# Moving the first output projection of each layer ahead of the attention of the following query tiles

## The chip, the cores and the metric

The kernel runs on one core of one Trainium2 chip. The metric is the device time of one execution in microseconds (us). The engines are called PE (matrix multiply; PEld is its weight load), DVE, ACT and POOL (elementwise work) and SP (the queue from which this kernel issues its data transfers). All inputs and the result lie in the device's main memory.

## The reference: what is computed

A two-layer transformer trunk over 1024 latent tokens and 256 context tokens, width 1024. Each layer has two halves.

First half: normalise (RMS) and modulate the tokens, project them (`w_in`), and compute three groups of mixers side by side. Group A is a gated mix within chunks of 128 positions. Group B is attention of 8 query heads in a window of 128 positions to each side, plus the context. Group C is differential attention: 4 heads, each with two softmax maps over all 1280 keys, whose difference weights the values. The three outputs are concatenated and go through one output projection (`w_out`), gated and added to the tokens:

```python
x = x + g1 * (jnp.concatenate([out_a, out_b, out_c], axis=-1) @ w_out[i])
x = x + g2 * conv_ffn(modulate(rms_norm(x, norm2_g[i]), sh2, sc2), w_up[i], conv_w[i], conv_b[i], w_down[i])
```

Second half: normalise again, then a gated MLP with 2816 inner channels and a convolution of width 3 along the tokens. Context tokens run through layer 0 in full, and in layer 1 only as keys and values.

## The kernel before, in words

**Tokens and groups.** A tile is 128 tokens: 0 to 7 are latent, 8 and 9 context. Attention works on pairs of tiles: (0,1), (2,3), (4,5), (6,7) and, in layer 0, (8,9). The output projection and the MLP work on three token groups per layer. In layer 0, `G0[0]` is tile 0 and the context (384 columns), `G0[1]` is tiles 1 to 3, `G0[2]` is tiles 4 to 7. In layer 1, `G1[0]` is tiles 0 and 1 (256 columns), `G1[1]` is tiles 2 to 4, `G1[2]` is tiles 5 to 7.

**Attention.** `attn_b(L, pair)` is group B for one pair of tiles: two units, one for each key head. `attn_c(L, hd, pairs)` is group C for one head and a list of pairs: one unit for each pair. It loads the head's keys and values once for the list (`Kc`, `Vc`). A unit of C runs, for each of its two tiles and two maps, three score matmuls into the accumulator tile `S` (L679), the running maximum on DVE (L483), the exponential on ACT (L682); then per tile the difference of the two maps on DVE (L689); then transposes into `T` (L714), copies to `PT` (L716) and the value matmuls into `O` (L705). The copy `on<-O` (L725) comes once per unit, so its count tells how many C units are done. For B, the transposes are L596, the value matmuls L606, and `ob<-O` (L619) comes once per unit. Each unit stores its result into the array `o_s` in main memory. There is one `O` tile, two `S` tiles and four tiles for exponentials.

**Output projection and norms.** `prep(L, G, ...)` takes one token group: it reads `o_s` back into `oT` in four parts (L786; the first part is group A, the next two are B, the last is C), loads `w_out` in eight slices of 128 output channels, runs 24 matmuls per slice (8 row blocks times 3 terms; L130, `z<-oT,wsp`), adds into `xg` (L807), and then normalises each 128 tokens: square on ACT (L200), sums on DVE (L203, L204), the power on POOL (L211), scaling on DVE (L217), modulation on ACT (L227), splitting into two parts (L228, L109). The MLP of that group can begin when all its norms are there.

**MLP.** `mlp(L, G, ...)` runs 22 steps f. Each loads two slices of `w_up`, runs `z<-h,wsp` matmuls, convolution and gate, and ends in `g<-t` (L864, once per step). The down projection (`z<-g,wsp`) of four finished steps is put between. All weights, of `w_out`, `w_up` and `w_down` alike, pass through the same three raw and three split buffers (`raw`, `wsp`), and projections and MLP share the same two accumulator tiles `z`.

**The order.** The program text is not the order on the engines. A scheduler that simulates the program picks, for each engine, the ready instruction that stands first in the text, and the resulting order on each engine is fixed. Text order is therefore a rank: what stands earlier wins when both are ready, and what stands later fills in. During the MLP of one group a hook at step f issues `prep` of the next group: `HK = (16, 13, 20, 12)`, so in layer 0 `prep(0, G0[1])` ranks in the middle of step 16 of the first MLP, and in layer 1 `prep(1, G1[1])` in the middle of step 20. Four steps ahead of that its `oT` loads are put into the text one by one.

Around the change, layer 0 has: the input projection with the attention of (8,9) and (0,1); then B and C of (2,3); `prep` of `G0[0]`; B and C of (4,5) and (6,7); the MLP of `G0[0]`. Layer 1 has: the input projection with the attention of (0,1); B and C of (2,3) and (4,5); `prep` of `G1[0]`; B and C of (6,7); the MLP of `G1[0]`.

Of the kernel before, what the change touches and what calls it, by code (L numbers as in the profile page):

```python
# [52 lines left out]
def trunk(ctx: ExitStack, tc: tile.TileContext, a: dict):  # L53
# [3 lines left out]
    def mkpool(name, bufs, side="left", space=None):  # L57
        kw = {"space": space} if space is not None else {}
        return tc.alloc_tile_pool(name=name, bufs=bufs, side=side, reuse_waits="tile", **kw)
# [51 lines left out]
    def wunit(src, nk, ncol, ws=ws, eng=dve):  # L111
        raw = wr.tile([P, nk, ncol], F32, tag="raw", name="raw")
        sp.dma_start(out=raw, in_=src.rearrange("(k p) c -> p k c", p=P))
        hl = ws.tile([P, 2, nk, ncol], F32R, tag="ws", name="wsp")
        act.activation(out=hl[:, 0], in_=raw, func=AF.Copy)  # L115
        if eng is pool and nk * ncol > 256:
            for k in range(nk):
                sub(eng, hl[:, 1, k], raw[:, k], hl[:, 0, k])
        else:
            sub(eng, hl[:, 1], raw, hl[:, 0])  # L120
        return hl

    def mm3(ps, w, h, nk, stat_w=True, first=True, last=True):

        for k in range(nk):
            for q, (i, j) in enumerate(TERMS):
                s = first and k == 0 and q == 0
                e = last and k == nk - 1 and q == 2
                if stat_w:
                    pe.matmul(ps, w(i, k), h(j, k), start=s, stop=e)  # L130
                else:
                    pe.matmul(ps, h(i, k), w(j, k), start=s, stop=e)  # L132
# [98 lines left out]
    def norm_tile(L, which, src, s, hi, lo, mkps, mkbig, f=None, ss=None, eng=pool, add='a'):  # L231
        norm_back(L, which, norm_front(src, mkps, mkbig, f, ss), s, hi, lo, eng, add)
# [536 lines left out]
    def attn_b(L, tiles, at, mkS, mkT, mkO):  # L769
        attend(units_b(L, tiles, at, mkS, mkT, mkO))  # L770

    def attn_c(L, hd, groups, at, mkS, mkT, mkO):
        attend(units_c(L, hd, groups, at, mkS, mkT, mkO))


    def prep_loads(L, G, p):

        wd = G["W"]
        xg = p.tile([P, KT, wd], F32, tag="xg", name="xg", bufs=1)
        oT = p.tile([P, 2, KT, wd], F32R, tag="h", name="oT", bufs=1)  # L780

        def load(k):
            for (xc, n, pieces) in G["op"]:
                for (tok, o, m, s) in pieces:
                    for h in range(2):
                        sp.dma_start(out=oT[:, h, k:k + 2, xc + o:xc + o + m].bitcast(F32),  # L786
                                     in_=o_s[L][h, k * P:k * P + 2 * P, tok:tok + m].rearrange("(c p) t -> p c t", p=P))

        return xg, oT, [lambda k=k: load(k) for k in range(0, KT, 2)]

    def prep(L, G, p, mp, pl=None, lo=dve):

        wd = G["W"]
        xg, oT, loads = pl or prep_loads(L, G, p)
        while loads:
            loads.pop(0)()
        if G["xh"]:
            dve.tensor_copy(xg[:, :, 0], xh)
        for (xc, n, pieces) in G["op"]:
            for ct in range(KT):  # L800
                w = wunit(a["w_out"][L][:, ct * P:ct * P + P], KT, P, eng=lo)
                ps = mkz()
                mm3(ps[:, :n], lambda j, k: w[:, j, k, :], lambda j, k: oT[:, j, k, xc:xc + n], KT)
                for (tok, o, m, s) in pieces:
                    xs = xg[:, ct, xc + o:xc + o + m]
                    sp.dma_start(out=xs, in_=x_s[:, ct, tok:tok + m])
                    dve.scalar_tensor_tensor(out=xs, in0=ps[:, o:o + m], scalar=mods[:, L, 16 + ct, s:s + 1], in1=xs,  # L807
                                             op0=ALU.mult, op1=ALU.add)
        hT = p.tile([P, 2, KT, wd], F32R, tag="h", name="h2", bufs=1)
        if G["xh"]:  # L810
            dve.tensor_copy(hT[:, :, :, 0:2], hal.bitcast(F32))
        big = lambda: mp.tile([P, KT, P], F32, name="nb", tag="nb", bufs=2)
        for i, (xc, hc, s) in enumerate(G["norm"]):
            norm_tile(L, 1, xg[:, :, xc:xc + P], s, hT[:, 0, :, hc:hc + P], hT[:, 1, :, hc:hc + P], mkU, big,
                      add=AN[L])

        def halo():
            if G["halo"] is not None:
                hc, xc = G["halo"]
                dve.tensor_copy(hal, hT[:, :, :, hc:hc + 2].bitcast(F32))  # L820
                dve.tensor_copy(xh, xg[:, :, xc])

        return xg, hT, halo
# [71 lines left out]
    def finish(L, G, xg, mp):  # L895
        if L < DEPTH - 1:
            for ct in range(KT):
                for (tok, xc, n) in G["out"]:
                    sp.dma_start(out=x_s[:, ct, tok:tok + n], in_=xg[:, ct, xc:xc + n])
            return  # L900
        for (tok, xc, n) in G["out"]:
            for o in range(0, n, P):
                m = min(P, n - o)
                ot = mp.tile([P, KT, P], F32, name="ot", tag="nb", bufs=2)
                for g in range(2):
                    px = mkT()
                    for k in range(4):
                        pe.transpose(px[:m, k * P:k * P + P], xg[:, 4 * g + k, xc + o:xc + o + m], ident)
                    if g:
                        dve.tensor_copy(ot[:m, 4:8], px[:m].rearrange("p (k t) -> p k t", k=4))  # L910
                    else:
                        act.activation(out=ot[:m, 0:4], in_=px[:m].rearrange("p (k t) -> p k t", k=4), func=AF.Copy)
                m16 = m - m % 16
                for r0, r1 in ((0, m16), (m16, m)):
                    if r1 > r0:
                        sp.dma_start(out=a["out"][0, tok + o + r0:tok + o + r1, :],
                                     in_=ot[r0:r1].rearrange("p k t -> p (k t)"))
# [15 lines left out]
    G1 = [dict(id="a", xh=False, W=256, op=[(0, 256, [(0, 0, 256, 0)])], norm=[(0, 0, 0), (128, 128, 0)],  # L933
               halo=(254, 255), segs=[(0, 256, [(0, 256, 0, 255, 0, 0)])], out=[(0, 0, 255)]),
          dict(id="b", xh=True, W=386, op=[(1, 384, [(256, 0, 384, 0)])], norm=nrm(3), halo=(384, 384),
               segs=[(0, 386, [(0, 386, 1, 385, 0, 0)])], out=[(255, 0, 384)]),
          dict(id="c", xh=True, W=386, op=[(1, 384, [(640, 0, 384, 0)])], norm=nrm(3), halo=None,
               segs=[(0, 386, [(0, 386, 1, 386, 0, 0)])], out=[(639, 0, 385)])]
# [13 lines left out]
    def mkz():  # L952
        zc[0] += 1
        if zc[1] and zc[0] % 2:
            return psS.tile([P, 512], F32, tag="S", name="zS")
        return psD.tile([P, 512], F32, tag="z", name="z")
# [103 lines left out]
    def attn(L, tiles):  # L1060
        for t in tiles:
            attn_b(L, t, at, mkS, mkT, mkO)
        for hd in range(4):
            attn_c(L, hd, tiles, at, mkS, mkT, mkO)
# [9 lines left out]
    M = mkpool("M0", 2, "right")  # L1074
    X2 = mkpool("X2", 1, "right")
    X1 = mkpool("X1", 1, "right")
    attn(0, [(2, 3)])
    x1 = prep(0, G0[0], X1, M)
    attn(0, [(4, 5), (6, 7)])

    def hook(f):
        ahead(0, G0[1], X2, f, HK[0], "x2")
# [2 lines left out]
    finish(0, G0[0], x1[0], M)  # L1085
    X1.release()
    at.release()
# [17 lines left out]
    M = mkpool("M1", 2, "left")  # L1105
# [52 lines left out]
    M = mkpool("M2", 2, "right")  # L1158
    X2 = mkpool("X5", 1, "right")
    X1 = mkpool("X4", 1, "right")  # L1160
    for t in A1[0]:
        attn_b(1, t, at, mkS, mkT, mkO)
    for hd in range(4):
        attn_c(1, hd, A1[0], at, mkS, mkT, mkO)
    x1 = prep(1, G1[0], X1, M)
    for t in A1[1]:
        attn_b(1, t, at, mkS, mkT, mkO)
    for hd in range(4):
# [6 lines left out]
    finish(1, G1[0], x1[0], M)  # L1175
    X1.release()
    at.release()
# [65 lines left out]
```

## Time and profile before

| | us |
|---|---|
| median of 3 runs | 3356.69 |
| lowest and highest | 3352.62, 3362.18 |
| the profiled execution | 3354.95 |
| its span, first to last instruction | 3353.1 |
| PE busy (94% of the span) | 3164.3 |
| DVE busy (70%) | 2342.6 |
| ACT busy (52%) | 1744.9 |
| POOL busy (26%) | 883.6 |

In the views, a group of instructions is written as line, engine, operation, tile written and tiles read. "x24" is a count. A window is a stretch of the span in us; for each engine it gives the busy time in it and the number of instructions. PEclk is the share of PE's full clock that was granted there. Matmuls overlap each other, so the busy time of PE counts a stretch once even where it is filled thinly.

### The profile page before, as it was taken

What the parts mean: (1) busy time and instruction counts of PE and PEld (TensorE: products, weight loads), DVE (VectorE), ACT (ScalarE), POOL (GpSimd) and SP (SyncE); (2) the same over time, 40 slices, a digit from 0 to 9 for tenths busy, and PEclk for the clock granted to TensorE, in tenths of its full rate; (3) what the DMA queues carried; (4) which work ended last, traced back from release to release, by engine and by line L of the source; (5) the groups of instructions that cost most, each with busy time, mean ns of one, the idle gap of its engine ahead of it and who ended that gap; (6) DMA issues with size and microseconds to landing.
All of it is one profiled execution on the core that took longest, in us unless ns stands there. A gap on an engine that the chain in (4) does not pass through costs nothing. (4 is left out here: it accounts for less than half of the span.)

```text
span 3353.1 us, 54588 instructions
## 1 busy us (share of the span) xinstructions
PE 3164.3 (94%) x19503; PEld 2753.6 (82%) x19503; DVE 2342.6 (70%) x5306; ACT 1744.9 (52%) x3059; POOL 883.6 (26%) x1170
## 2 busy tenths in 40 slices
PE   6999998999999899999999899999999989999999
PEld 3777556887888798989999777666887779999998
DVE  5776756756878785878677678647786685666666
ACT  3555546555555653646444345556665564454443
POOL 1545211222233550128001154222322323222000
PEclk8999999999999999999999899999999999999999
DMA  8655777344542853378243556445645446434433
GB/s 259 194 156 162 223 248 186 89 121 124 136 116 83 255 154 110 103 207 242 87 117 112 160 149 161 126 139 136 167 135 149 122 118 189 120 111 135 137 114 108
DMA packets 754127, 499.52 MB, mean 149 GB/s; under 512 B 81480, under 2 KB 697792, under 8 KB 753856
## 3 DMA queue, kind: packets, MB, share of 16 engines
q1 hardware_dynamic: 753856, 496.03, 51.7%
q8 instruction: 155, 2.54, 0.3%
q14 instruction: 116, 0.95, 0.1%
HBM read 432.48 MB, written 63.44 MB: 148 GB/s over the span
## 5 line engine op out<-in xcount | busy, mean ns | idle before, releaser
L130 PE MATMUL z<-h,wsp 128*128 128x386 f32 (+3 forms) x5280 | 871.7, 318 | 20.4 <-DVE t L854 10.2
L130 PEld LDWEIGHTS z<-h,wsp 128*128 128x128 f32 x5280 | 822.0, 190 | 36.4 <-issue 13.9
L115 ACT ACTIVATE wsp<-raw 128x1024 fp32r<-128x1024 f32 (+2 forms) x660 | 555.9, 845 | 442.1 <-PE z L130 179.0
L109 DVE TENSOR_TENSOR wsp<-raw,wsp 128x1024 fp32r<-128x1024 f32 (+2 forms) x516 | 565.9, 1099 | 121.3 <-ACT wsp L115 118.5
L130 PE MATMUL z<-g,wsp 128*128 128x386 f32 (+3 forms) x2640 | 463.5, 323 | 17.8 <-ACT wsp L115 5.7
L130 PEld LDWEIGHTS z<-g,wsp 128*128 128x128 f32 x2640 | 418.1, 192 | 35.8 <-issue 11.0
L132 PE MATMUL z<-wsp,h 128*128 128x512 f32 x1584 | 404.8, 402 | 13.0 <-ACT wsp L115 3.3
L109 POOL TENSOR_TENSOR wsp<-raw,wsp 128x128 fp32r<-128x128 f32 x528 | 253.9, 513 | 448.8 <-ACT wsp L115 397.2
L132 PEld LDWEIGHTS z<-wsp,h 128*128 128x128 f32 x1584 | 291.6, 191 | 79.9 <-ACT wsp L115 4.3
L130 PE MATMUL zS<-h,wsp 128*128 128x386 f32 (+1 forms) x2112 | 333.7, 313 | 8.1 <-DVE t L854 3.2
L130 PEld LDWEIGHTS zS<-h,wsp 128*128 128x128 f32 x2112 | 318.9, 190 | 10.9 <-ACT wsp L115 4.3
L847 ACT ACTIVATE t<-z,cw 128x386 f32<-128x386 f32 (+3 forms) x220 | 137.8, 627 | 209.8 <-PE z L130 208.6
L851 DVE SCALAR_TENSOR_TENSOR t<-z,cw,t 128x255 f32<-128x255 f32 (+3 forms) x264 | 132.5, 502 | 144.6 <-ACT t L847 144.2
L682 ACT ACTIVATE ec<-ec,nmc 128x1280 f32<-128x1280 f32 (+1 forms) x144 | 182.1, 1265 | 52.1 <-DVE ec L483 51.0
L170 POOL TENSOR_TENSOR mev<-mev,mtr 128x512 f32<-128x512 f32 x112 | 175.8, 1583 | 124.6 <-ACT mtr L169 121.7
L130 PE MATMUL z<-oT,wsp 128*128 128x384 f32 (+2 forms) x1056 | 200.0, 336 | 4.9 <-DMA oT<-o_s 3.4
L130 PE MATMUL zS<-g,wsp 128*128 128x386 f32 (+1 forms) x1056 | 184.4, 319 | 14.9 <-ACT wsp L115 4.3
L483 DVE TENSOR_SCALAR_CACHE_REDUCE ec<-S,nmc 128x512 f32<-128x512 f32 (+1 forms) x256 | 156.7, 612 | 56.0 <-PE S L679 52.7
L879 DVE SCALAR_TENSOR_TENSOR xg<-z,mods,xg 128x384 f32<-128x384 f32 (+5 forms) x288 | 140.4, 501 | 75.8 <-PE z L130 74.7
L130 PEld LDWEIGHTS z<-oT,wsp 128*128 128x128 f32 x1056 | 176.1, 188 | 15.1 <-issue 4.9
L370 POOL TENSOR_TENSOR rs<-ss,cst 128x8 f32<-128x8 f32 (+1 forms) x76 | 119.5, 1572 | 259.5 <-DVE ss L368 187.7
L579 POOL TENSOR_SCALAR dgb<-cst,ls 128x128 f32<-128x128 f32 x144 | 89.2, 632 | 372.7 <-PE T L616 182.3
(248 smaller groups left out, 4848.1 us busy)
## 6 DMA issues: line engine op xcount, KB each, us to landing
raw<-in_w_up_dram SPq DMA_DIRECT2D x264, 512.0 KB
mraw<-in_w_ada_dram SPq DMA_DIRECT2D x96, 512.0 KB
raw<-in_w_down_dram SPq DMA_DIRECT2D x192, 256.0 KB
Kc<-qk_s SPq DMA_DIRECT2D x96, 320.0 KB
raw<-in_w_in_dram SPq DMA_DIRECT2D x52, 512.0 KB
raw<-in_w_out_dram SPq DMA_DIRECT2D x48, 512.0 KB
raw<-in_w_down_dram SPq DMA_DIRECT2D x104, 192.0 KB
qk_s<-st SPq DMA_DIRECT2D x18, 512.0 KB
```

The costliest lines, as they stand in the source:

```text
L109: eng.tensor_tensor(out=lo, in0=src, in1=hi.bitcast(F32), op=ALU.subtract)
L115: act.activation(out=hl[:, 0], in_=raw, func=AF.Copy)
L130: pe.matmul(ps, w(i, k), h(j, k), start=s, stop=e)
L132: pe.matmul(ps, h(i, k), w(j, k), start=s, stop=e)
L170: pool.tensor_tensor(out=acc[s], in0=acc[s], in1=pr, op=ALU.add)
L370: pool.tensor_tensor(out=rs[:, :ns], in0=ss[:, 1, :ns], in1=mhalf[:, :ns], op=ALU.pow)
L483: dve.tensor_scalar(out=neg, in0=s_ap, scalar1=-1.0, scalar2=init, op0=ALU.mult, op1=ALU.min, accum_out=acc)
L579: pool.tensor_scalar(out=dgs[ti][:, j], in0=ident, scalar1=ls[:, j:j + 1], scalar2=None, op0=ALU.mult)
L682: act.activation(out=e[:, :nk], in_=e[:, :nk], func=AF.Exp, scale=-1.0, bias=acc, accum_out=l1[:, m, ti:ti + 1])
L847: act.activation(out=t[:, o:o + n], in_=ps[:, :n], func=AF.Identity, scale=cw[:, L, 1, ft:ft + 1], bias=cw[:, L, 3, ft:ft + 1])
L851: dve.scalar_tensor_tensor(out=t[:, o + b + 1:o + e], in0=ps[:, b:e - 1], scalar=cw[:, L, 0, ft:ft + 1], in1=t[:, o + b + 1:o + e], op0=AL ...
L879: dve.scalar_tensor_tensor(out=xs, in0=ps[:, b + o0:b + o1], scalar=mods[:, L, 40 + ct, s:s + 1], in1=xs, op0=ALU.mult, op1=ALU.add)
```

## The change

In layer 0, `prep` of `G0[0]` moves ahead of the attention of (2,3), and the two calls of `attn` become one. With that the pair (2,3) joins the list of pairs: B now runs (2,3), (4,5), (6,7), and C runs, for each head in turn, (2,3), (4,5), (6,7). In layer 1, `prep` of `G1[0]` moves ahead of B and C of (2,3) and (4,5), whose own order stays.

```diff
-    attn(0, [(2, 3)])
     x1 = prep(0, G0[0], X1, M)
-    attn(0, [(4, 5), (6, 7)])
+    attn(0, [(2, 3), (4, 5), (6, 7)])
...
+    x1 = prep(1, G1[0], X1, M)
     for t in A1[0]:
         attn_b(1, t, at, mkS, mkT, mkO)
     for hd in range(4):
         attn_c(1, hd, A1[0], at, mkS, mkT, mkO)
-    x1 = prep(1, G1[0], X1, M)
     for t in A1[1]:
         attn_b(1, t, at, mkS, mkT, mkO)
```

The function that takes the list, in both versions:

```python
def attn(L, tiles):
    for t in tiles:
        attn_b(L, t, at, mkS, mkT, mkO)
    for hd in range(4):
        attn_c(L, hd, tiles, at, mkS, mkT, mkO)
```

## The prediction

> **What bounds the kernel now.** I read the page first, then the busy time by window around the two places of the change, then the counts of finished attention units, and last the chain of waits where a projection waits for attention. By the page PE sets the time, so a new order can only win or lose where PE is short of work:
>
> ```profile
> PE 3164.3 (94%) x19503; PEld 2753.6 (82%) x19503; DVE 2342.6 (70%) x5306; ACT 1744.9 (52%) x3059; POOL 883.6 (26%) x1170
> Kc<-qk_s SPq DMA_DIRECT2D x96, 320.0 KB
> ```
>
> The windows are: layer 0's first projection, its norms, its MLP up to the hook, layer 1's first norms, and the place in layer 1 where the second projection waits.
>
> ```profile
> core 0: us, PE busy (x) PEld busy (x) DVE busy (x) ACT busy (x) POOL busy (x), PEclk, DMA share, GB/s
> 487.00:560.00 73.00, 70.35 (x433) 54.14 (x433) 38.39 (x113) 37.75 (x66) 10.94 (x15) 1.00 0.77 209
> 560.00:602.00 42.00, 30.48 (x145) 19.54 (x144) 35.52 (x97) 30.81 (x60) 7.14 (x6) 0.72 0.57 142
> 605.00:912.00 307.00, 301.44 (x1876) 259.53 (x1875) 209.73 (x582) 168.52 (x306) 73.44 (x136) 0.99 0.44 119
> 2266.00:2302.00 36.00, 30.84 (x193) 18.88 (x191) 23.39 (x88) 26.60 (x54) 14.17 (x17) 0.91 0.58 156
> 2577.00:2596.00 19.00, 13.52 (x83) 8.75 (x81) 6.19 (x33) 7.30 (x18) 3.07 (x5) 0.82 0.51 146
> ```
>
> In the norms (560 to 602) PE has no MLP yet and is filled only with attention: 30.5 of 42 us busy at a clock of 0.72, while DVE is at 35.5. From 605 to 912 PE is full. At 2577 it is thin again. What happens there is the key to my forecast. The first view is PE's work on `oT` by window, the second its work on the MLP's `h`, the third the chain of waits:
>
> ```profile
> 487.00:560.00 73.00, 39.26 (x192) 33.10 (x192) 1.00 0.77 209
> 912.00:959.00 47.00, 36.51 (x192) 33.58 (x192) 1.00 0.44 119
> 2217.00:2266.00 49.00, 23.73 (x168) 21.54 (x168) 1.00 0.42 119
> 2567.00:2578.00 11.00, 7.25 (x36) 6.12 (x36) 1.00 0.37 109
> 2578.00:2595.00 17.00, 0.00 (x0) 0.00 (x0) 0.80 0.56 159
> ```
>
> ```profile
> 2568.00:2595.00 27.00, 0.00 (x0) 0.87 0.50 143
> ```
>
> ```profile
> 2589.51 2.07 DMA o_s<-stc
> 2591.60 0.38 SPq L786
> 2592.02 4.06 DMA oT<-o_s
> 2596.12 2.02 PE z L130 x10
> ```
>
> Layer 1's second projection starts with exactly 36 matmuls, two slices of 18. These are the row blocks of A and B, and they fill both `z` tiles. The last row blocks are C's, whose result is stored only at 2589.5, so the slices stop. From 2568 to 2595 **not one MLP matmul runs**: the MLP has work, but its rank is lower, and the held projection owns the weight buffers and the `z` tiles. So a hook whose attention isn't done doesn't just wait; it takes PE's filler away.
>
> **Layer 0, what the change moves.** The order of units was B(2,3) x2, C(2,3) x4, B(4,5) and (6,7) x4, C x8. The second projection (tiles 1 to 3) needs C of (2,3) for all heads: the first 6 units. After the change it is B x6, then for each head C(2,3), C(4,5), C(6,7). Head 3's C(2,3) is now **unit 16 of 18**. How far attention gets by the hook is read from the counts of `on<-O` (C) and then `ob<-O` (B), followed by that of the MLP steps:
>
> ```profile
> 490.00:605.00 115.00, 0.25 (x1) 0.90 0.69 182
> 605.00:912.00 307.00, 1.38 (x5) 0.99 0.44 119
> 912.00:1060.00 148.00, 1.08 (x4) 0.99 0.38 106
> ...
> 490.00:605.00 115.00, 1.20 (x2) 0.90 0.69 182
> 605.00:912.00 307.00, 2.38 (x4) 0.99 0.44 119
> ...
> 605.00:912.00 307.00, 7.79 (x15) 0.99 0.44 119
> ```
>
> By 912, when the hook's projection starts, 6 C and 6 B units are done, 12 of 18; 16 only by 1060. Beside the MLP 9 units take 307 us, 34 us each. After the change prep and norms outrank attention, so I take only B(2,3), 2 units, as done when the MLP begins; 9 more follow in the same MLP steps: 11 at the hook, **5 missing** (4 if the four units that are at or near their end at 605 now also get through, 5.5 if B(2,3) itself is late).
>
> What a missing unit costs: PE's own work per C unit, from the transposes, value matmuls and scores of the 8 units in 836 to 1113:
>
> ```profile
> 836.00:1113.00 277.00, 24.94 (x160) 18.04 (x160) 0.99 0.45 126
> 836.00:1113.00 277.00, 33.00 (x320) 21.40 (x320) 0.99 0.45 126
> 836.00:1113.00 277.00, 31.92 (x88) 16.06 (x88) 0.99 0.45 126
> ```
>
> (24.94 + 33.00 + 31.92) / 8 = 11.2 us. How long a unit takes without MLP beside it is not shown in a pure form. The nearest stretch is 560 to 602, whose groups are:
>
> ```profile
> L679 PE MATMUL S<-Kc,qc 128*128 128x512 f32 (+1 forms) x26 | 13.5, 547 | 9.0 <-DVE ec L483 8.8
> L689 DVE SCALAR_TENSOR_TENSOR ec<-ec,rho 128x1280 f32<-128x1280 f32 x4 | 6.2, 1550 | 0.1
> L211 POOL TENSOR_TENSOR nrs<-nms,cst 128x1 f32<-128x1 f32 x3 | 1.7, 564 | 21.9 <-DVE nms L209 21.9
> ```
>
> L689 runs once per tile, so 4 in 42 us are 2 units, 21 us each, with norms beside them on DVE. The lower bound is PE's own 11.2 us, where a hold costs nothing; the upper one is the 34 us beside the MLP. I take 21, because that stretch is like the hold in that PE has nothing else. A missing unit then costs 21 - 11.2 = 9.8 us of PE, 5 of them 49 us. The 36 matmuls that run ahead (7.25 us) are useful work in the hold: **42 us lost** (0 to 107 with both bounds of both numbers).
>
> **Layer 0, what the change gains.** The projection starts at 487 in either order, since its last inputs come then; 192 matmuls need 36.5 us undisturbed (the 912 row) and took 73 us beside B(2,3), which had the higher rank. Ranked first they end some 30 us sooner, but B's work is only deferred, so no time is won there. The gain is in the norms. There C(2,3) outranked them on DVE; POOL's power waited 21.9 us for DVE. PE needed 2 x 11.2 = 22.4 us for attention and lost up to 42 - 22 - 3 for the norms' own few matmuls = 17 us. After the change norms go first and B fills in, which brings more PE work per unit:
>
> ```profile
> 686.00:836.00 150.00, 25.64 (x152) 16.52 (x152) 0.99 0.45 120
> 686.00:836.00 150.00, 25.80 (x152) 8.06 (x152) 0.99 0.45 120
> ```
>
> 152 of 40 transposes each are 3.8 units, so 51.4 / 3.8 = 13.5 us without scores, against 7.2 for C counted likewise. I take **12 us won** (0 if B's chain is as thin as C's, 17 at most).
>
> **Transfers.** Moved with prep in layer 0 are 16 `oT` loads, 16 `xg` loads and 8 of `w_out`; in layer 1, 8 of each:
>
> ```profile
> L786 SPq DMA_DIRECT2D oT<-o_s x56: 359/468/2254, 430.8 to 2802.9; - x56
> L806 SPq DMA_DIRECT2D xg<-x_s x56: 319/430/1582, 446.8 to 2814.6; - x56
> ```
>
> At about 0.45 us of SP's queue each, 40 issues are 18 us and 24 are 11 us, now ahead of the `Kb`, `Vb` and `qb` loads of B(2,3) where those aren't out yet. Behind them wait B(2,3)'s scores. It costs PE nothing as long as the projection runs; what is late next is the attention, which the 5 missing units contain. The joint list of pairs loads a head's keys once instead of twice: 4 heads x 4 `Kc` loads of 96 fall away, 4 of V too. With DMA at 0.44 that is worth nothing by itself.
>
> **Layer 1.** The projection of tiles 0 and 1 ran at 2217 to 2266, 168 matmuls in 49 us against 168 x 0.19 = 32 us undisturbed: MLP work can start some 20 us earlier with the norms. PE lost 5 us at 2266; I take 5 won (0 to 10). In return B(2,3) falls back by about one unit, and the list of pairs is unchanged, so the hold at 2577, which exists already, gets longer by about one unit: 9.8 us lost (0 to 20). Net **+5 us** (-10 to +20).
>
> **Sum.** +42 - 12 + 5 = +35 us. The profiled execution took 3354.95 us, 1.85 more than its span, so 3390; against the median of 3356.69, which is 1.7 us above that execution, **3392 us**.
>
> **Rivals.**
>
> (a) *Faster: the hold costs nothing.* Attention alone on PE overlaps its units so well that one takes no more than about 14 us, or gets through 16 units by the hook. Then the hold costs at most 5 x 2.8 - 7 = 7 us, less than the 17 us of PE that the norms lose now, and layer 1 wins its 5. For it: DVE's longest work per unit is below PE's, and there are four tiles for exponentials. Against it: 9.0 us of idle PE before the scores, 8.8 of it for DVE's maximum, in the one stretch that resembles it. It gives 7 - 17 - 5 = -15, 3342. It decides once a unit alone takes under 14 us.
>
> (b) *No difference: the rank changes little.* The projection can't start before 487 and 2217 whatever its rank, the fillers just trade places, and a hold of two or three units (2.5 x 9.8 - 7 = 17 us) eats the 12 + 5 won. 3357. For it: PE was full in 487 to 560 and 605 to 912. Against it: unit 16 instead of unit 6.
>
> (c) *Dearer: the hold runs at a low clock.* The 42 us of the norms had a clock of 0.72, and the second half of them less:
>
> ```profile
> 580.00:600.00 20.00, 0.00 (x0) 0.00 (x0) 0.57 0.29 66
> ```
>
> The view of waits of those 42 us (total, times, longest):
>
> ```profile
> PE S L679 <- DVE ec L483: 8.8, 12, 2.9
> ```
>
> At 0.57 PE's share of a unit is 11.2 / 0.57 = 19.6 us instead of 11.2 / 0.72 = 15.6, so a unit takes 25: 5 x 13.8 - 7 = 62 lost, with -12 and layer 1 at its +12 again 62 in all, 3419. For it: the cause of the thin PE, scores that wait for DVE, is the same. Against it: the hold has no norms on DVE. [...]
>
> **Chances.** Forecast 0.50, (a) 0.18, (b) 0.15, (c) 0.17. The forecast by itself spans 3370 (4 units at 18 us: 20 - 12 + 5) to 3416 (5.5 units at 24 us: 63 - 12 + 8). Over the cases I give 3340 to 3436: it takes in (a) and (c) with some of their own spread, and leaves out the ends at which every bound adds up. A difference below 0.3%, 10 us, can't be told from none: faster 0.18, same 0.15, slower 0.67.
>
> **What would show it.** Right: in the changed profile `z<-oT` in layer 0 makes 36 matmuls somewhere near 880, then a gap of 80 to 120 us without `z<-h` or `z<-g`, with PE at half to two thirds busy and `on<-O` every 20 us or so, ended by `oT<-o_s` after `o_s<-stc`; the first norms end before 595 and PE is over 80% busy in them; layer 1's gap at 2577 grows. Wrong: no gap after the 36 matmuls (then (a)), a gap of under 50 us (then (b)), or MLP matmuls running inside the gap, which would make the hold itself false.

## The result and the profile after

The changed kernel takes 3385.74 us (median of 4 runs, 3375.55 to 3388.08), against 3354.65 us for the kernel before on the same chip (median of 4 runs). The ratio is 1.0083, 95% interval 1.0056 to 1.0110: 31 us slower by the medians, 28 by the ratio. The forecast was 3392 us, 35 us slower. Of all runs below, one of ten in experiment 5 (3504 us at a granted clock of 0.84) and one of four in experiment 11 (4239 us at 0.66) fell into a slow state that the other runs of their kernels don't show, and they are left out of the medians.

The profiled execution took 3388.08 us with a span of 3386.3, 33.2 us more than before. The page of the changed kernel, engine totals:

```profile
PE 3187.3 (94%) x19503; PEld 2764.0 (82%) x19503; DVE 2345.2 (69%) x5306; ACT 1748.5 (52%) x3059; POOL 885.8 (26%) x1170
```

The same 19503 matmuls, and 23 us more of "busy" PE: the same work done thinly. Where, is told by PE's work on `oT` by window (PE, PEld, granted clock, DMA share, GB/s):

```profile
902.00:912.00 10.00, 7.17 (x36) 6.23 (x36) 1.00 0.74 177
912.00:1015.00 103.00, 0.00 (x0) 0.00 (x0) 0.75 0.15 39
1015.00:1053.00 38.00, 29.07 (x156) 27.02 (x156) 1.00 0.26 74
```

Layer 0's second projection issues 36 matmuls and then stands still for **103 us**. In the kernel before, its 192 matmuls ran in one piece in 912 to 958. During this hold there isn't one MLP matmul. The view of PE's work on `h` and that of its work on `g` have the same line:

```profile
912.00:1015.00 103.00, 0.00 (x0) 0.75 0.15 39
```

The next view is the work of all engines in layer 0's first projection, its norms, the MLP up to the hook, the hold, layer 1's first norms, and the stop of layer 1's second projection:

```profile
core 0: us, PE busy (x) PEld busy (x) DVE busy (x) ACT busy (x) POOL busy (x), PEclk, DMA share, GB/s
487.00:543.00 56.00, 46.04 (x254) 40.31 (x254) 20.69 (x51) 15.94 (x26) 3.11 (x5) 0.94 0.69 203
543.00:595.00 52.00, 44.28 (x272) 30.06 (x270) 31.19 (x110) 39.48 (x84) 20.80 (x24) 0.90 0.37 102
605.00:902.00 297.00, 292.20 (x1813) 248.36 (x1813) 218.87 (x593) 169.79 (x300) 68.81 (x128) 1.00 0.42 113
912.00:1015.00 103.00, 78.54 (x408) 50.01 (x407) 66.25 (x199) 52.42 (x97) 3.49 (x5) 0.75 0.15 39
2278.00:2302.00 24.00, 20.61 (x124) 12.83 (x122) 17.93 (x70) 16.11 (x34) 9.60 (x12) 0.86 0.41 110
2601.00:2624.00 23.00, 17.14 (x123) 11.93 (x122) 7.67 (x38) 10.24 (x24) 3.44 (x6) 0.93 0.42 116
```

PE is 78.5 of 103 us busy at a clock of 0.75, DVE at two thirds, DMA nearly empty, so no engine is full. Of PE's 24.5 idle us, 16.3 are waits of the scores for DVE's maximum (the line is in the last section): attention units follow one another at the pace of their own chain. The counts of finished units show the progress (first `on<-O` of C, then `ob<-O` of B):

```profile
605.00:902.00 297.00, 1.09 (x4) 1.00 0.42 113
902.00:1016.00 114.00, 1.54 (x6) 0.78 0.20 51
912.00:1015.00 103.00, 1.28 (x5) 0.75 0.15 39
...
490.00:605.00 115.00, 1.15 (x2) 0.93 0.53 153
605.00:902.00 297.00, 2.36 (x4) 1.00 0.42 113
```

At 902 there are 6 B and 4 C units done, 10 of the 16 needed. Of the six that are missing, one ends before 912 and five in the hold. The result of the sixteenth is stored at 1008.4 (`o_s<-stc`) and read back from 1011.2 (`oT<-o_s`), and the projection goes on at 1015.6.

**The balance.** Between marks in the two traces (first and last `z<-oT` of each projection, first MLP matmul, last input projection of layer 1, last matmul), after against before: from the first projection's start to the MLP's start 101 against 115 us; MLP to the hook's projection 312 against 310; that projection 150 against 46; from its end to the start of the third 281 against 335; on to the end of layer 1's input projection 849 against 846; from there to the end 1201 against 1211. So -14 + 2 + 104 - 54 + 3 - 10 = +31 us, and 2 us before all that. The 54 us come back where attention is over by then: of C units, one ends between the second and the third projection, against five before.

```profile
958.00:1293.00 335.00, 1.33 (x5) 0.97 0.51 153
```

```profile
1052.00:1334.00 282.00, 0.28 (x1) 0.99 0.58 173
```

### The profile page after: what moved, and what is told of

Read it like the earlier page. It is cut to its first block, busy times and chain, and to the rows that moved or that the text cites. A ratio compares the mean times of both kernels' runs of the same rounds, so it can differ in the third digit from the quotient of the medians.

```text
span 3386.3 us, 54583 instructions
## 1 busy us (share of the span) xinstructions
PE 3187.3 (94%) x19503; PEld 2764.0 (82%) x19503; DVE 2345.2 (69%) x5306; ACT 1748.5 (52%) x3059; POOL 885.8 (26%) x1170
## 5 line engine op out<-in xcount | busy, mean ns | idle before, releaser
L130 PE MATMUL z<-g,wsp 128*128 128x386 f32 (+3 forms) x2640 | 455.6, 321 | 15.9 <-DVE t L854 4.9
L130 PEld LDWEIGHTS z<-g,wsp 128*128 128x128 f32 x2640 | 416.5, 191 | 31.1 <-issue 9.9
L170 POOL TENSOR_TENSOR mev<-mev,mtr 128x512 f32<-128x512 f32 x112 | 182.7, 1646 | 121.6 <-ACT mtr L169 118.6
L130 PE MATMUL z<-oT,wsp 128*128 128x384 f32 (+2 forms) x1056 | 195.9, 338 | 13.5 <-DMA oT<-o_s 11.3
L130 PE MATMUL zS<-g,wsp 128*128 128x386 f32 (+1 forms) x1056 | 183.6, 318 | 11.2 <-DVE t L854 3.1
L679 PE MATMUL S<-Kc,qc 128*128 128x512 f32 (+1 forms) x400 | 157.4, 418 | 26.6 <-DVE ec L483 24.3
```

Source lines behind the costliest of these rows:

```text
L170: pool.tensor_tensor(out=acc[s], in0=acc[s], in1=pr, op=ALU.add)
L679: pe.matmul(S[:, :w_], q[:, m, ti * P:ti * P + P], K[m][:, o:o + w_], start=True, stop=True)
```

## The experiments

Each kernel is compared with runs of the kernel before on its own chip; differences are between medians. My theory was the hold; the rivals were the rank itself (attention late everywhere) and layer 1.

**1. Layer 0's part alone.**

```diff
-    attn(0, [(2, 3)])
     x1 = prep(0, G0[0], X1, M)
-    attn(0, [(4, 5), (6, 7)])
+    attn(0, [(2, 3), (4, 5), (6, 7)])
```

> Layer 0 as changed, layer 1 as before. My theory: the loss is the hold of layer 0's second projection, from 911 to 1015 us in the changed kernel, where PE has attention alone. This kernel keeps the whole hold, so it is slower by 35 to 45 us, at least as much as the whole change. Rival 1: the loss comes from the other order in both layers in general (attention late everywhere); then this kernel has about half of it, 15 us. Rival 2: the loss sits in layer 1; then it is within 10 us of before.

Measured: 3395.71 against 3350.08, 1.0138 (1.0110 to 1.0166), +45.6 us. The loss is all in layer 0, and more than the whole change. Its trace has the same hold, without a matmul on `oT`, `h` or `g`.

**2. Layer 1's part alone.**

```diff
+    x1 = prep(1, G1[0], X1, M)
     for t in A1[0]:
         attn_b(1, t, at, mkS, mkT, mkO)
     for hd in range(4):
         attn_c(1, hd, A1[0], at, mkS, mkT, mkO)
-    x1 = prep(1, G1[0], X1, M)
```

> Layer 0 as before, layer 1 as changed. My theory: no new hold of note, so -10 to +5 us; the traces of before and changed suggest about -7, since layer 1 starts its output projection 40 us late in the changed kernel and ends 33 us late. Rival 1 (loss by order in general): +15 us. Rival 2 (loss sits in layer 1): +30 us.

Measured: 3343.23 against 3350.08, 0.9983 (0.9971 to 0.9995), -6.8 us. Layer 1 wins a little: the difference is under the 10 us that the forecast asked for, but the interval leaves out 1, and the traces agree. From the end of layer 1's input projection to the last matmul, the four kernels with layer 1 as before (the kernel before and experiments 1, 3 and 5) take 1207 to 1211 us, and all with the changed order 1189 to 1206. Its own hold did get longer, as the forecast said. This is what all engines do in it:

```profile
2559.00:2590.00 31.00, 23.34 (x149) 15.68 (x150) 10.91 (x56) 13.27 (x31) 6.18 (x10) 0.89 0.33 94
```

It takes 31 us instead of some 18, with two matmuls of the projection in it, and PE is filled to a similar share (23.3 of 31 us against 13.5 of 19). Behind the needed unit stand B units of the last pair, and DVE is busy for only 11 of the 31 us. PE's busy share alone doesn't set this hold apart from layer 0's (0.75 against 0.76); the granted clock does (0.89 against 0.75). What this hold costs by itself isn't shown.

**3. Projection in front in layer 0, (2,3) a list of its own.** Rank without the joint list.

```diff
-    attn(0, [(2, 3)])
     x1 = prep(0, G0[0], X1, M)
+    attn(0, [(2, 3)])
     attn(0, [(4, 5), (6, 7)])
```

> Layer 0 only: the projection is ranked ahead of the attention of (2,3), but (2,3) stays a list of its own, so its group C is again units 3 to 6 and not 3, 6, 9 ... 16. My theory: rank alone doesn't cost, the joint list does. No hold at the hook; the norms run with less idle PE: -17 to 0 us, my value -10. Rival (the rank itself costs, since it delays attention): +20 us or more.

Measured: 3353.60 against 3350.08, 1.0010 (0.9998 to 1.0022), +3.5 us: no difference by the bound of 0.3%. The hold is gone, the second projection runs in one piece:

```profile
900.00:949.00 49.00, 36.41 (x192) 33.45 (x192) 1.00 0.40 108
```

So the rank itself isn't the loss; the rival of experiment 1 falls. But the gain that I had expected in the norms isn't there either. Busy time by window, this kernel (projection, then norms):

```profile
480.00:541.00 61.00, 52.06 (x304) 44.40 (x302) 24.27 (x60) 19.23 (x31) 3.10 (x5) 0.92 0.74 209
541.00:586.00 45.00, 37.83 (x211) 21.60 (x210) 32.98 (x100) 36.76 (x72) 12.79 (x15) 0.88 0.47 117
```

and the kernel before:

```profile
480.00:558.00 78.00, 75.97 (x487) 58.37 (x484) 42.40 (x126) 40.41 (x72) 10.94 (x15) 1.00 0.77 209
558.00:602.00 44.00, 31.68 (x150) 20.04 (x148) 37.38 (x102) 32.67 (x61) 7.14 (x6) 0.73 0.58 147
```

The norms' idle PE falls from 12 to 7 us, but the projection's rises from 2 to 9. The views of PE's waits in 480 to 545 say why, this kernel first, then before (total, times, longest):

```profile
PE z L130 <- DMA oT<-o_s: 8.3, 5, 6.9
```

```profile
PE z L130 <- DMA oT<-o_s: 1.9, 3, 1.2
```

The projection makes 36 matmuls and then waits 6.9 us for the last part of `oT`. Ranked first, its matmuls stand ahead of B(2,3) in PE's queue. Before, it stopped after 36 matmuls too (496.7 to 505.5), but B(2,3) covered that wait. The same 10 us, this kernel first, then before:

```profile
500.00:510.00 10.00, 2.89 (x14) 2.49 (x14) 0.43 (x4) 0.78 (x2) 0.00 (x0) 0.67 1.01 277
```

```profile
500.00:510.00 10.00, 10.00 (x69) 6.46 (x68) 4.47 (x19) 6.13 (x11) 0.00 (x0) 1.00 0.89 261
```

**4 and 7. The whole change with another hook in layer 0.** Step 20, then step 12, instead of 16. This changes the length of the hold and leaves the rank of attention as it is.

```diff
-HK = (16, 13, 20, 12)
+HK = (20, 13, 20, 12)
```

> The whole change, with layer 0's second projection hooked at MLP step 20 instead of 16. My theory: four more steps at 19 us each give attention 2.3 more units beside the MLP (34 us each) before the hook, so 2.7 units are missing instead of 5, the hold is about 55 us instead of 104, and the time falls by 2.3 x 10 = 23 us against the changed kernel, to about +8 us against before. Rival (the loss isn't the hold): unchanged, +31 us.

```diff
-HK = (16, 13, 20, 12)
+HK = (12, 13, 20, 12)
```

> The whole change with layer 0's second projection hooked at MLP step 12 instead of 16. My theory: in the changed kernel 9 units are done at that time, 7 of the 16 are missing, and at 19 us each the hold is about 135 us against 104. With hook 20 (hold 69 us, +22.7) and hook 16 (104 us, +33 over its runs) the time grows by 0.31 us per us of hold, so +43 us. Rival (the loss isn't the hold): +31 us, unchanged, or less, since the second projection comes earlier.

Measured: hook 20, 3372.80 against 3350.08, 1.0069 (1.0042 to 1.0095), +22.7 us; hook 12, 3405.85 against 3353.05, 1.0150 (1.0134 to 1.0166), +52.8 us. The holds, from PE's work on `oT`, hook 20 and hook 12:

```profile
982.00:1050.00 68.00, 0.00 (x0) 0.00 (x0) 0.77 0.15 37
```

```profile
836.00:982.00 146.00, 0.00 (x0) 0.00 (x0) 0.74 0.16 40
```

In neither does an MLP matmul run. Holds of 68, 103 and 146 us go with +22.7, +31.1 and +52.8 us. From 68 to 146 that is 0.39 us per us of hold; the slope is rough, since the intervals reach 5 to 9 us to each side. It fits the price of a unit: 103 us for 5 units is 20.6 us each, of which PE needs 11.2, so 0.46 of the hold is lost to PE. My numbers on record were 55 us of hold for hook 20 (68 measured) and 135 for hook 12 (146), so attention gets about half a unit less far than I had counted. The times on record, +8 and +43 us, were both too low, by 15 and 10 us: the loss falls less with a shorter hold, and grows more with a longer one, than I had put down.

**5. C of (2,3) before the others.** All three pairs stay behind the projection and B runs as in the change, but the needed unit is the tenth instead of the sixteenth.

```diff
-    attn(0, [(2, 3)])
     x1 = prep(0, G0[0], X1, M)
-    attn(0, [(4, 5), (6, 7)])
+    for t in [(2, 3), (4, 5), (6, 7)]:
+        attn_b(0, t, at, mkS, mkT, mkO)
+    for ps_ in [[(2, 3)], [(4, 5), (6, 7)]]:
+        for hd in range(4):
+            attn_c(0, hd, ps_, at, mkS, mkT, mkO)
```

> Layer 0 only: the projection in front and B of all three pairs first, as in the change, but C of (2,3) for all four heads before C of (4,5) and (6,7). The needed unit is then number 10 of 18 instead of 16. My theory: at the hook 10 to 11 units are done, so there is hardly any hold (0 to 20 us), and the time is that of the kernel with the separate list, +3 us, between -5 and +12. Rival (the loss is that the attention of all three pairs is put behind the projection, whatever its own order): as with the joint list alone, +45 us.

Measured: 3347.52 against 3353.06, 0.9981 (0.9969 to 0.9992), -5.5 us, with no hold:

```profile
901.00:947.00 46.00, 37.34 (x192) 33.39 (x192) 1.00 0.41 112
```

Its counts of finished units up to there, C and then B:

```profile
605.00:901.00 296.00, 1.09 (x4) 0.99 0.49 131
...
490.00:605.00 115.00, 1.14 (x2) 0.93 0.53 150
605.00:901.00 296.00, 2.35 (x4) 0.99 0.49 131
```

It has 6 B and 4 C units done at 901, as the changed kernel has at 902. What differs is which 4: here they are the four heads of (2,3). (It also loads each head's keys twice again, 112 loads of `Kc` against 96, which is more work and not less.) Moving the same units within the same rank is worth 51 us against experiment 1.

**6 and 12. Both projections in front, (2,3) a list of its own.** The whole change without its joint list, run on two chips. The edit is against the changed kernel:

```diff
     x1 = prep(0, G0[0], X1, M)
-    attn(0, [(2, 3), (4, 5), (6, 7)])
+    attn(0, [(2, 3)])
+    attn(0, [(4, 5), (6, 7)])
```

> Both layers' projections in front, (2,3) of layer 0 as a list of its own: the change without its joint list. My theory: the sum of the two parts measured, +3.5 - 6 = -3 us (-9 to +3); it is also the point without a hold in layer 0 on the line of hold length against time. Rival (the parts don't add, since layer 1 only wins back what layer 0 lost): +3 us or more.

> The kernel with both projections in front and (2,3) a list of its own once more, on another chip and with more rounds: its -20 us (0.9941) was 17 more than the sum of its parts. If the sum is right and that was the chip: -3 us, between -9 and 0. If layer 1 wins more behind the new layer 0: -20 us again.

Measured: 3332.76 against 3353.05, 0.9941 (0.9922 to 0.9961), -20.3 us, and again 3335.89 against 3353.36, 0.9948 (0.9935 to 0.9962), -17.5 us. The sum of the parts, +3.5 - 6.8 = -3 us, was wrong, the rival of +3 us or more as well, and it wasn't the chip. By the marks above, layer 1 from the end of its input projection takes 1189 and 1190 us here, 1203 in experiment 2 and 1211 before. The text of layer 1 is the same as in experiment 2, but the scheduler orders each engine anew behind another layer 0. Of the 13 to 14 us, 9 to 10 lie in the second projection with its hold (84 and 85 us against 94) and 3 after the third one's start (474 against 477). Why the order comes out better here isn't shown. It is also part of why the line of experiments 4 and 7 can't be drawn on to a hold of nothing: that would be at -4 us, and in those kernels and the changed one the stretch takes 1200 to 1202 us.

**9 and 10. Layer 1's hook one step later**, in the kernel of experiment 2 (layer 1's change alone) and in that of experiment 6. Against these kernels the edit is:

```diff
-HK = (16, 13, 20, 12)
+HK = (16, 13, 21, 12)
```

> A candidate for a version faster than both: layer 0 as before, layer 1's projection in front, and layer 1's second projection hooked at MLP step 21 instead of 20. My theory: the kernel with layer 1 alone has a hold of 31 us at that hook (2558 to 2590); one step later (about 19 us) it shrinks to about 10 us, and at 0.31 us per us that is 6 us more won: -12 us against before (-18 to -5). Rival (PE finds other work in that hold, since group B of the last pair is dense): -6 us, as with layer 1 alone.

> Both projections in front, (2,3) a list of its own, and layer 1's second projection hooked at step 21 instead of 20. My theory from the run of layer 1 alone at hook 21 (-8 us, against -7 at hook 20): the hold in layer 1 costs little, since group B of the last pair fills it; so the time stays within 6 us of the same kernel at hook 20 (measured -20, run again beside it). Rival (that hold costs like the one in layer 0): 8 to 10 us faster than at hook 20.

Measured: 3345.03 against 3353.05, 0.9972 (0.9961 to 0.9984), -8.0 us against -6.8 at step 20; and 3339.68 against 3353.36, 0.9957 (0.9944 to 0.9971), -13.7 us against -17.5. In the traces the stop of the second projection shrinks from 31 to 11 us and from 24 to 10. A shorter hold in layer 1 brings nothing that these runs can tell.

**11. Experiment 5's layer 0 and the changed layer 1.**

> Both projections in front, all three pairs' B first, then C of (2,3), then C of the rest. My theory: parts add, -5 (layer 0 so) and -7 (layer 1 alone): -12 us against before, -18 to -5. Rival (layer 1 wins more behind a layer 0 with its projection in front, as the -20 of the kernel with the separate list suggests): -20 us or more.

Measured: 3319.54 against 3353.36, **0.9908 (0.9893 to 0.9924), -33.8 us** by the median of three runs (3319.38 to 3329.10), 26 to 36 us by the interval. It beats both kernels. The sum of the parts (-12) was wrong again, by 22 us; its layer 1 takes 1189 us from the end of the input projection, as in experiment 6. PE's total on its page is 17 us below that of the kernel before:

```profile
PE 3147.5 (95%) x19503; PEld 2746.7 (83%) x19503; DVE 2338.1 (70%) x5306; ACT 1744.1 (53%) x3059; POOL 878.7 (26%) x1170
```

## Why the prediction was right, and where it wasn't

**The hold: right in mechanism, place and size.** Needed unit 16 instead of 6; 36 matmuls, then a gap without any MLP matmul, ended by `oT<-o_s` after `o_s<-stc`: all as the forecast describes. Expected were 80 to 120 us near 880; it is 103 us from 912. Experiments 1, 3 and 5 show that the loss comes from the order of C's units in the joint list and neither from the rank nor from layer 1; experiments 4 and 7 show that the time follows the hold's length. The numbers behind it: 34 us per unit beside the MLP (8 units in 297 us, 37 measured); 21 us alone (20.6); 11 units done (10 at the hook, 11 when the hold begins); 49 us of PE lost in the hold (103 - 5 x 11.2 = 47). One sign was missed: PE was to be half to two thirds busy in the hold, and it is 0.76. That the held projection keeps the MLP out through both the weight buffers and the two `z` tiles is read from the program; which of the two would do it alone was not tried.

**Slips in its sums.** The 7 us taken off for the 36 matmuls are not to be taken off: these ran from 902 to 912, ahead of the 103 us, so 47 stands against the 42 of the sum. The bound of 107 us goes with 5 missing units; with 5.5 it is 118. The 11.2 us per unit counts 88 scores for 8 units, which at 12 each have 96; with all of them it is 11.6. Rival (c) takes layer 1 at +12 us and doesn't say from where.

**The gain in the norms: wrong.** The step was "12 us won", with the remark that no time is won or lost in the projection itself. Experiment 3 shows 5 us won in the norms and 7 lost in the projection, which, ranked first, holds PE's queue for 6.9 us while its last part of `oT` is under way. So it ends 16 us sooner in the changed kernel and not some 30. It is the same mechanism as the hold, on a small scale, and the forecast had its rows: layer 1's second projection in the kernel before also stops after 36 matmuls for `oT`. The row of POOL's wait for DVE that I took as a sign of delayed norms says little: in the changed kernel the norms rank ahead of all attention and still take 48 us from the projection's last matmul to the MLP's first, against 44 before. Two of the signs came true without the gain: the norms ended before 595, with PE 85% busy in them.

**Layer 1: wrong sign.** The step was +5 us. Measured is -6.8 alone, and 10 us less from the input projection to the end within the whole change. I priced a hold that grows by a whole unit, some 20 us, at layer 0's 9.8 us. In the changed kernel its stop grew only from 18 to 24 us, in experiment 2 to 31, and experiments 9 and 10 find no price for it. The gain's side was misread as well: the 0.19 us per matmul came from a group of 384 columns, but this one has 256, and its 168 matmuls took 25 us in the changed kernel, not 32. From the end of the input projection to the first MLP matmul it is 125 us there against 160 before, so 35 us sooner and not some 20. What each side is worth in time isn't shown.

**The sum** came out near (+35 forecast, +31 measured) because these errors have opposite signs: layer 0 alone costs 46 us (experiment 1) where the sum had +30, and layer 1 gives 7 to 15 us where it had +5 lost. That the total is right within 4 us is luck; that it is a loss of tens of us is not.

**Rivals.** (a), a hold that costs nothing, holds at most in layer 1. (b), no difference, is what the rank alone gives in layer 0 (experiment 3). (c), a dearer hold at a low clock: the clock was 0.75, near the 0.72 of the stretch from which I took the 21 us, so it was in the price already.

## What to carry to other kernels

In a program ordered by rank, ask of each block that is moved which later block needs its result and in what place of the new order that result comes; merging lists of work can push the one needed result to the end even where the total work is less. A consumer that ranks ahead of the filler work and shares its buffers doesn't just wait when its input is late, it takes the filler away, so its price is what PE can't do in that time. In layer 0 it was 0.4 to 0.5 us per us of hold (0.39 between the two hooks, 51 us for some 103 between experiments 1 and 5); in layer 1, where other units were left, a hold shorter by 14 to 20 us brought nothing. Effects of two moves in such a program need not add: here they differed from their sum by 14 to 22 us.

## What the runs showed of the hardware that I had not expected

In the hold the granted clock isn't a steady 0.75. Windows inside it show it going to and fro between half and full:

```profile
927.00:936.00 9.00, 7.44 (x33) 5.09 (x33) 5.01 (x16) 4.97 (x8) 0.70 (x1) 0.50 0.07 15
937.00:946.00 9.00, 6.09 (x37) 3.34 (x35) 7.11 (x21) 4.69 (x10) 0.00 (x0) 1.00 0.10 29
947.00:956.00 9.00, 7.45 (x34) 5.14 (x35) 4.62 (x13) 4.79 (x8) 0.70 (x1) 0.50 0.23 57
957.00:963.00 6.00, 5.48 (x35) 3.12 (x34) 4.34 (x15) 3.09 (x8) 0.00 (x0) 1.00 0.15 42
```

Half and full come round every 20 us or so, about as long as one unit takes. The longest wait of PE in the whole hold is 2.0 us (view of PE's waits in 912 to 1015: total, times, longest):

```profile
PE S L679 <- DVE ec L483: 16.3, 16, 2.0
```

So the clock falls to 0.50 in a stretch without any wait of PE above 2.0 us. A thinly filled stretch stands ahead of the falls in these windows: PE is busy for 2.03 of the 5 us of 922 to 927 and for 2.25 of the 5 us of 942 to 947, and in the 5 us after each the clock is 0.50. Whether that brings the fall, and how thin it has to be, isn't shown. The busy time of PE in these windows is no measure of its work: the 7.4 busy us of the first window, at half clock, hold 33 matmuls, and the 6.1 of the second, at full clock, hold 37. The mix differs, but so does the time of one kind alone: a value matmul (`O<-PT,Vc`, L705) takes 431 ns on average in the first window and 285 in the second.
